# Moving two products of a later group of columns beside page building, with squares in PSUM, split exponentials and reordered pools

## The chip, the cores and the metric

The kernel runs on one core of one Trainium2 chip. A core has five engines with a queue of instructions each: TensorE (PE in the profile) multiplies matrices and transposes, VectorE (DVE), ScalarE (ACT) and GpSimd (POOL) work element by element, and SyncE (SP) issues most of the transfers. An engine works its queue in order: an instruction whose operand is not there yet holds up all that stand behind it. The metric is device microseconds (us) of one execution; lower is better. Before the change three runs gave 2585.85 to 2589.04 us, with a median of 2587.65 us.

## The reference

One layer of an encoder with 2048 tokens of 1024 features. In float32 throughout:

```python
h = rms_norm(x, norm_mix)
z = h @ w_in                       # 1024 x 4352: q_A k_A v_A q_B k_B v_B gate_A gate_B
y_a = windowed_gqa(q_a, k_a, v_a, sink)        # 8 heads, window |t-s| <= 128, ALiBi, a sink logit
y_b = neighborhood_attn(q_b, k_b, v_b, rpb)    # 8 heads on a 32 x 64 grid, 8 x 16 neighbours, bias
gates = sigmoid([g_a, g_b] + b_gate)
x = x + (gates[:, :1024] * (y_a @ w_proj_a) + gates[:, 1024:] * (y_b @ w_proj_b)) @ w_out
x = x + relu(rms_norm(x, norm_mlp) @ w_up) ** 2 @ w_down
out = rms_norm(x, norm_final)
```

## The kernel before

Tokens are worked in four blocks of 512. Every float32 operand of a product is split into a high and a low part (a cast on ACT writes the high part, a subtraction on DVE the low part, L309 and L310 in `split`), and a product is three passes on PE: high x high, high x low, low x high (`mm3s`, L313 to L315). So each operand that PE takes has one ACT cast and one DVE subtraction of its own ahead of it.

**The head, 0 to about 360 us.** The product `h @ w_in` of the first two blocks is done by a scheme with seven products in place of eight, numbered 1, 2, 5, 6, 7, 4, 3 in the order in which they are made (`ORDER`). The columns of `w_in` are taken in nine groups (`QUADS`, counted from 0; the code calls a group a quad): 0 is k_A and v_A, 1 is q_A, 2 is q_B, 3 is k_B, 4 is v_B, 5 to 8 are the gates. `in_quad` is a generator; each `next` makes one of the seven products of its group, into PSUM banks named x (products 1 and 2), z (5 and 3) and y (6, 7, 4). Product 1 is copied out as `c1` (tile zc, L514), and the result of product 2 is the first finished tile (q and k tiles are written as ze, L455 to L460).

The right-hand operands of the products are pages (tiles zh1 to zh7): pages 1 and 2 are the two halves of the first block's normalised, transposed tokens, page 3 belongs to the second block, and pages 5, 6, 7 and 4 are sums and differences of both. While the second block's pages are built (transposes on PE, L301; scaling on ACT, L534; four combining instructions on DVE, L537), only products 1 and 2 can run, since they need the first block alone. Before the change products 1 and 2 of groups 0, 1 and 2 run there; then come the products 5, 6, 7, 4 and 3 of groups 0 and 1, alternating; after that one group follows the other in a loop over q.

The weights come from DRAM: 1 MB halves (zraw, two tiles of four rotating buffers each) or, for group 2's first two products, 512 KB pieces loaded into buffers of the first block's token tiles (xin). `in_left` makes the sums and parts of the weights (zS, zwhl), ahead of the products that use them.

The norms: `rstd_shared` (blocks 0 and 1) sums the squares of half a row on ACT (L236) and of the other half on DVE (L238), with the squares themselves going to scratch tiles in SBUF; `rstd_of` (blocks 2 and 3, within groups 5 and 6) sums both halves on ACT with the squares going to the two PSUM banks of `tpool` (L250), adds them on DVE (L253) and takes the power on POOL (L255).

**Attention A, about 360 to 611 us.** Units of 128 queries of one key group; `turn` transposes a chunk of probabilities on PE, ACT casts it (tile ph, L874 or L879) and DVE makes the low part (L875 or L880); `product` multiplies it with v (tile av, L896). `score` of a unit three ahead multiplies q and k (L821), adds the bias and takes the maximum on DVE (L825), and after the fourth score ACT makes two small instructions and four exponentials of 288 columns (L829 to L832) in one row. DVE adds the sums and takes reciprocals (L833, L834), and POOL scales (L836). Between the chunks stand feature products of blocks 2 and 3 (mm, L203 to L205) as a filler, in steps of three matmuls, spread evenly by the constants `STEP` and `SCORE`.

**Attention B, from about 600 us.** The same pattern with units of 16 columns of the grid. Bias tiles biass0, biass1 and biasl are made on POOL from raw rows braw and the masks (L1033). Queries are loaded into qb0, qb1, qb2. The pools of B are laid on a stack of memory in the order of a list of names (L1007); a tile whose memory overlaps memory of A's tiles waits until these are done with. The scheduler keeps the order of the code within an engine except where `tc.issue_after` or priorities of the framework move an instruction behind another one.

## Time and profile before

| what | value |
|---|---|
| runs | 2585.85 to 2589.04 us, median 2587.65 us |
| the profiled execution | 2586.27 us, of which the span of the profile is 2584.4 us |
| PE busy | 2557.0 us, 99% of the span, 12200 instructions |
| DVE, ACT, POOL busy | 1610.0 us (62%), 1235.5 us (48%), 401.6 us (16%) |
| granted TensorE clock | 0.9 or more in all 40 slices of the page |
| DMA | 490.40 MB, mean 190 GB/s |

The page shows shares of the whole span. A view by windows gives the busy time of each engine in a stretch, a view of waits lists, for each engine, on which other engine's instruction its idle time ended, and the chain follows the work that ended last. Durations of matmuls in the views are longer than the distance from one start to the next, since matmuls are pipelined; where the prediction counts PE time it uses distances between starts.

### The profile page before, as it was taken

The page shows a single profiled execution, that of the slowest core. Times are in us where ns is not written, and L with a number is a line of the kernel's source. Part 1 is how long each engine was busy: PE and PEld are TensorE (multiplying, and loading weights), DVE is VectorE, ACT ScalarE, POOL GpSimd, SP SyncE. Part 2 cuts the span into 40 slices and gives each one's busy share as a digit, 9 for nine tenths or more (in the row PEclk, how much of TensorE's full clock was granted, in tenths as well). Part 3 has the DMA queues.
Part 4 walks back from the last instruction along what each step waited for, and adds up shares of the span by engine and source line. Part 5 has one row for each costly group of instructions (what it writes and reads, how often), then busy time and mean ns, then how long its engine had stood idle before and what let it go on. Part 6 is the DMA issues. An engine that isn't in the chain of part 4 may idle for free.

```text
span 2584.4 us, 34858 instructions
## 1 busy us (share of the span) xinstructions
PE 2557.0 (99%) x12200; PEld 2141.6 (83%) x12200; DVE 1610.0 (62%) x2625; ACT 1235.5 (48%) x2265; POOL 401.6 (16%) x613
## 2 busy tenths in 40 slices
PE   8999999999999999999999999999999999999999
PEld 6888888888888888888888888888888888888887
DVE  8776657765544445566578767866665535554766
ACT  5334347775555555443335554654454322323454
POOL 1000026665455541000000000100000000000010
PEclk9999999999999999999999999999999999999999
DMA  5657486467867647675457666844428835444555
GB/s 185 198 163 208 129 262 174 121 188 200 225 192 203 187 131 236 218 226 171 128 175 240 226 210 212 305 162 163 151 108 310 283 102 183 143 155 159 188 195 171
DMA packets 354127, 490.40 MB, mean 190 GB/s; under 512 B 28808, under 2 KB 188808, under 8 KB 351776
## 3 DMA queue, kind: packets, MB, share of 16 engines
q1 hardware_dynamic: 346896, 471.14, 58.4%
q10 hardware_dynamic: 7056, 17.04, 1.8%
q8 instruction: 96, 1.57, 0.3%
q14 instruction: 79, 0.65, 0.1%
HBM read 328.64 MB, written 159.45 MB: 189 GB/s over the span
## 4 chain that ended last, share of the span: by engine, by line
PE 87%; DMA 5%; DVE 4%; ACT 2%; issue 1%; SPq 1%; POOL 0%; ACTq 0%; POOLq 0%; DVEq 0%
PE b L313 16%; PE b L314 16%; PE b L315 16%; PE mm L203 5%; PE mm L205 5%; PE mm L204 5%; PE pt L203 2%; PE pt L204 2%; PE av L1128 2%; PE pt L205 2%; PE zb L315 2%; PE zb L313 2%; PE zb L314 2%; PE pt L1107 2%; PE s L1076 2%; PE av L896 1%
## 5 line engine op out<-in xcount | busy, mean ns | idle before, releaser
L314 PE MATMUL b<-dwh,dah 128*128 128x512 f32 x896 | 348.5, 389 | 0.0
L315 PE MATMUL b<-dwh,dah 128*128 128x512 f32 x896 | 347.6, 389 | 0.0
L313 PE MATMUL b<-dwh,dah 128*128 128x512 f32 x896 | 339.6, 389 | 0.0
L309 ACT CAST dah<-da 128x1024 fp32r<-128x1024 f32 (+1 forms) x128 | 120.9, 945 | 368.1 <-PE b L315 244.1
L310 DVE TENSOR_TENSOR dah<-da,dah 128x1024 fp32r<-128x1024 f32 (+1 forms) x128 | 139.5, 1090 | 223.4 <-ACT dah L309 223.3
L314 PE MATMUL b<-ubh,uwhlb 128*128 128x512 f32 x592 | 230.3, 389 | 0.0
L313 PE MATMUL b<-ubh,uwhlb 128*128 128x512 f32 x592 | 230.2, 389 | 0.0
L315 PE MATMUL b<-ubh,uwhlb 128*128 128x512 f32 x592 | 229.2, 389 | 0.0
L203 PE MATMUL mm<-hT,whl 128*128 128x512 f32 x544 | 218.5, 402 | 1.3 <-DVE zc L304 1.2
L205 PE MATMUL mm<-hT,whl 128*128 128x512 f32 x544 | 213.6, 393 | 0.0
L204 PE MATMUL mm<-hT,whl 128*128 128x512 f32 x544 | 213.1, 392 | 0.0
L313 PEld LDWEIGHTS b<-dwh,dah 128*128 128x128 f32 x896 | 168.2, 188 | 35.0
L314 PEld LDWEIGHTS b<-dwh,dah 128*128 128x128 f32 x896 | 168.2, 188 | 34.9
L315 PEld LDWEIGHTS b<-dwh,dah 128*128 128x128 f32 x896 | 168.2, 188 | 34.9
L313 PE MATMUL zb<-zh,zwhl 128*128 128x512 f32 x476 | 186.2, 393 | 5.2 <-DVE zh L537 1.6
L314 PE MATMUL zb<-zh,zwhl 128*128 128x512 f32 x476 | 185.8, 390 | 0.0
L315 PE MATMUL zb<-zh,zwhl 128*128 128x512 f32 x476 | 183.0, 390 | 1.7 <-DVE zwhl L310 1.7
L304 DVE TENSOR_TENSOR uc<-b,uc 128x512 f32<-128x512 f32 x160 | 109.1, 689 | 104.5 <-PE b L315 103.5
L1679 POOL TENSOR_TENSOR st<-st,power 128x1 f32<-128x1 f32 x16 | 13.4, 844 | 925.2 <-DVE st L1678 925.2
L313 PEld LDWEIGHTS b<-ubh,uwhlb 128*128 128x128 f32 x592 | 111.1, 188 | 23.5 <-issue 0.4
L314 PEld LDWEIGHTS b<-ubh,uwhlb 128*128 128x128 f32 x592 | 111.1, 188 | 23.1
L315 PEld LDWEIGHTS b<-ubh,uwhlb 128*128 128x128 f32 x592 | 111.1, 188 | 23.0
(269 smaller groups left out, 5883.1 us busy)
## 6 DMA issues: line engine op xcount, KB each, us to landing
at<-uc SPq DMA_DIRECT2D x224, 256.0 KB
da<-at SPq DMA_DIRECT2D x96, 512.0 KB
dw<-in_w_down_dram SPq DMA_DIRECT2D x160, 256.0 KB
uraw<-in_w_up_dram SPq DMA_DIRECT2D x32, 1024.0 KB
raw<-in_w_in_dram SPq DMA_DIRECT2D x34, 512.0 KB
zraw<-in_w_in_dram SPq DMA_DIRECT2D x16, 1024.0 KB
z<-zg SPq DMA_DIRECT2D x64, 256.0 KB
zg<-zc SPq DMA_DIRECT2D x32, 256.0 KB
```

What stands on the lines that cost most here:

```text
L203: PE.matmul(ps, lh, rh, start=first, stop=False)
L204: PE.matmul(ps, lh, rl, start=False, stop=False)
L205: return PE.matmul(ps, ll, rh, start=False, stop=last).ins
L304: return eng.tensor_tensor(out=out, in0=a, in1=b, op=op).ins
L309: casts.append(A.copy(hi, src).ins)
L310: return eng.tensor_tensor(out=lo, in0=src, in1=hi.bitcast(F32), op=ALU.subtract).ins
L313: PE.matmul(ps, lh, rh, start=first, stop=False, skip_group_check=True)
L314: PE.matmul(ps, lh, rl, start=False, stop=False, skip_group_check=True)
L315: PE.matmul(ps, ll, rh, start=False, stop=last, skip_group_check=True)
L1076: ins = PE.matmul(ps[:, :n], self.q[:, i, :], kv[:, z, B_R0[i] // 4 : (B_R0[i] + B_NR[i]) // 4, 4 * B_C0[j] : 4 * (B_C0[j] + w)], start=z ...
L1107: ins = PE.transpose(pt[:kp, at + (i - i0) * P : at + (i - i0 + 1) * P], self.s[i][:, rr : rr + kp], ident).ins
L1128: ins = PE.matmul(po[:, i0 * P : (i0 + ni) * P], self.v[:kp, c, :], src[:kp, o : o + ni * P], start=pair == x == z == 0, stop=(c == 7 and ...
```

## The change

Five edits.

1. In `rstd_shared` the squares go to the two PSUM banks of `tpool` in place of two SBUF scratch tiles, whose pools are dropped.
2. Products 1 and 2 of group 3 (the k_B columns) are made beside the second block's pages too: their two weight pieces are loaded early into xin buffers, product 1 after the pages' first half, product 2 after the second. Their `c1` tiles go to a ring zc3 of their own, which is kept until group 5.
3. In `rstd_of` the DVE addition of blocks 2 and 3 becomes two additions on POOL, with EPS held in a tile. In group 6 the squares of the last two token tiles are put behind the sixth weight cast, not the fifth.
4. In attention A the four exponentials of a unit are taken in two halves (`weigh`), each placed behind the cast and the low part of the chunk transposed next; the sums, reciprocals and scaling follow the second half.
5. In the list of B's pools qb1 and qb2 stand ahead of biass1.

```diff
     sink_t = cp.tile([P, AH], F32, name="sink_t")
-    power = cr.tile([P, 1], F32, name="power")
+    half = cr.tile([P, 2], F32, name="power")
+    power, eps = half[:, 0:1], half[:, 1:2]
     G.memset(power, -0.5)
+    G.memset(eps, EPS)
...
         st = T(pl, [P, 4], F32, "st", 4)
-        junk = T(pl, [P, 512], F32, "junk", 1)
+        junk = zbank(tpool, 2)
         A.activation(junk, t[:, 0:512], AF.Square, accum_out=st[:, 0:1])
-        other = T(pl, [P, 512], F32, "junkv", 1)
+        other = zbank(tpool, 2)
...
         r = st[:, 2 : 3]
-        V.scalar_tensor_tensor(out=r, in0=st[:, 0:1], scalar=EPS if mean else D * EPS, in1=st[:, 1:2],
-                               op0=ALU.add, op1=ALU.add)
+        if mean:
+            G.tensor_tensor(out=r, in0=st[:, 0:1], in1=st[:, 1:2], op=ALU.add)
+            G.tensor_tensor(out=r, in0=r, in1=eps, op=ALU.add)
+        else:
+            V.scalar_tensor_tensor(out=r, in0=st[:, 0:1], scalar=D * EPS, in1=st[:, 1:2], op0=ALU.add, op1=ALU.add)
...
     in_page[3] = ring(s_z, "zh3", PAGE, F32R, 2)
+    s_c = ExitStack()
+    in_c3 = ring(s_c, "zc3", [P, BT], F32, 2)
...
     kvw = ring(s_kv, "kvw", [P, 4, 256], F32, 2)
-    xp.update(pools(s_kv, "right", ("junk", "junkv", "st"), "x0"))
+    xp.update(pools(s_kv, "right", ("st",), "x0"))
...
-    def in_quad(c, w, lf, right, ybanks=ypool, zbanks=zpool):
+    def in_quad(c, w, lf, right, ybanks=ypool, zbanks=zpool, kept=None):
...
                 if n == 1:
-                    c1[a] = in_c()
+                    c1[a] = (kept or in_c)()
...
-    ops2 = []
-
-    def operands2():
+    ops = {2: [], 3: []}
+
+    def operands(q):
         while True:
-            yield ops2.pop(0)
-
-    quad2 = in_quad(*QUADS[2], operands2(), right)
-    for p in range(2):
-        t = T(xp, [P, D], F32, "xin", 8).rearrange("p (k c) -> p k c", k=4)
-        c = QUADS[2][0]
-        SY.dma_start(t, w_in[0][p * BT : (p + 1) * BT, c : c + 256].rearrange("(k p) f -> p k f", p=P))
-        ops2.append(left_parts(t, 256, V))
-        if p == 0:
-            with tc.issue_after(last_part[0]):
-                for o, h, l in zip(halves(t1), *map(halves, right[1])):
-                    add(V, o, h.bitcast(F32), l.bitcast(F32))
-        next(quad2)
+            yield ops[q].pop(0)
+
+    quads = {q: in_quad(*QUADS[q], operands(q), right, kept=in_c3 if q == 3 else None) for q in (2, 3)}
+    early = {}
+    for q in (2, 3):
+        c = QUADS[q][0]
+        for p in range(2):
+            t = T(xp, [P, D], F32, "xin", 8).rearrange("p (k c) -> p k c", k=4)
+            SY.dma_start(t, w_in[0][p * BT : (p + 1) * BT, c : c + 256].rearrange("(k p) f -> p k f", p=P))
+            early[q, p] = t
+
+    def first_two(q, p):
+        ops[q].append(left_parts(early[q, p], 256, V))
+        next(quads[q])
+
+    ops[2].append(left_parts(early[2, 0], 256, V))
+    with tc.issue_after(last_part[0]):
+        for o, h, l in zip(halves(t1), *map(halves, right[1])):
+            add(V, o, h.bitcast(F32), l.bitcast(F32))
+    next(quads[2])
+    first_two(2, 1)
...
                 page_parts(5, t1, V)
+                first_two(3, 0)
...
             scaled_less(l, ps, k, h.bitcast(F32))
+    first_two(3, 1)
...
             s_v.close()
+            s_c.close()
...
         del casts[:]
-        lf = list(in_left(ws, 256, (1, 2) if q == 2 else ()))
+        lf = list(in_left(ws, 256, (1, 2) if q in quads else ()))
...
                 normalised(xp, xt, Junk(), by_scalar=True)
-        ops2.extend(lf if q == 2 else ())
-        for n, _ in enumerate(quad2 if q == 2 else in_quad(*QUADS[q], iter(lf), right)):
+        if q in quads:
+            ops[q].extend(lf)
+        for n, _ in enumerate(quads[q] if q in quads else in_quad(*QUADS[q], iter(lf), right)):
             if q == 6 and n == 0:
-                for t, behind in zip(xt, 2 * [copied[0]] + 2 * [casts[4]]):
+                for t, behind in zip(xt, 2 * [copied[0]] + 2 * [casts[5]]):
...
+    cast, low = [None], [None]
+
+    def behind_parts():
+        both = ExitStack()
+        for ins in (cast[0], low[0]):
+            both.enter_context(tc.issue_after(ins))
+        return both
+
...
-        def score(self, u, forced=True):
+        def score(self, u, forced=True, later=False):
...
                                    scale=1.0, scalar=sink_g, op0=ALU.add, op1=ALU.max, accum_out=mx[:, u : u + 1])
-            if u < 3:
+            if u == 3 and not later:
+                self.weigh((0, 1))
+                self.weigh((2, 3))
+
+        def weigh(self, us):
+            s = self.s
+            mx, nm, sm, es, ri = (self.st[:, k, :] for k in range(5))
+            sink_g = sink_p[:, self.g : self.g + 1]
+            if us[0] == 0:
+                A.activation(nm, mx, AF.Copy, scale=-1.0)
+                A.activation(es, mx, AF.Exp, bias=sink_g, scale=-1.0)
+            for u in us:
+                lo, hi = self.span[u]
+                A.activation(s[:, u, lo:hi], s[:, u, lo:hi], AF.Exp, bias=nm[:, u : u + 1], accum_out=sm[:, u : u + 1])
+            if us[0] == 0:
                 return
-            A.activation(nm, mx, AF.Copy, scale=-1.0)
-            A.activation(es, mx, AF.Exp, bias=sink_g, scale=-1.0)
-            for u, (lo, hi) in enumerate(self.span):
-                A.activation(s[:, u, lo:hi], s[:, u, lo:hi], AF.Exp, bias=nm[:, u : u + 1], accum_out=sm[:, u : u + 1])
...
             if kind == "rest":
-                A.copy(ph[0:64, at], pt[0:64, at])
-                V.tensor_tensor(out=ph[64:P, at], in0=pt[0:64, at], in1=ph[0:64, at].bitcast(F32), op=ALU.subtract)
+                cast[0] = A.copy(ph[0:64, at], pt[0:64, at]).ins
+                low[0] = V.tensor_tensor(out=ph[64:P, at], in0=pt[0:64, at], in1=ph[0:64, at].bitcast(F32), op=ALU.subtract).ins
...
             pl = T(ap_, [P, 512], F32R, "pl", 2)
-            A.copy(ph[:, at], pt[:, at])
-            V.tensor_tensor(out=pl[:, at], in0=pt[:, at], in1=ph[:, at].bitcast(F32), op=ALU.subtract)
+            cast[0] = A.copy(ph[:, at], pt[:, at]).ins
+            low[0] = V.tensor_tensor(out=pl[:, at], in0=pt[:, at], in1=ph[:, at].bitcast(F32), op=ALU.subtract).ins
...
     chunks = [(n, c) for n, x in enumerate(units) for c in x.groups()]
-    behind, scored, begin = [], 0, given
+    behind, weighed, scored, begin = [], [], 0, given
...
         behind.append((x, c, x.turn(c)))
+        if weighed:
+            with behind_parts():
+                y, us = weighed.pop(0)
+                y.weigh(us)
...
             for u in {"middle": (0, 1), "outer": (2, 3), "rest": ()}[c]:
-                units[n + AHEAD].score(u)
+                units[n + AHEAD].score(u, later=True)
                 scored += 1
+                if u == 3:
+                    weighed = [(units[n + AHEAD], us) for us in ((0, 1), (2, 3))]
...
     s_b = ExitStack()
-    bp = pools(s_b, "right", ("masks", "kb0", "qb0", "braw0", "biass0", "stb", "biass1", "qb1", "qb2", "braw1", "biasl", "kb1"), "b")
+    bp = pools(s_b, "right", ("masks", "kb0", "qb0", "braw0", "biass0", "stb", "qb1", "qb2", "biass1", "braw1", "biasl", "kb1"), "b")
...
     last_exp, last_parts, n_raw, n_short = [None], [None], [0], [0]
```

The first place is the head, where DVE has finished the first half of the second block's pages. The names zh1, zh2 are pages of the first block, zh3, zh5, zh6, zh7 and zh4 those that need the second block; zwhl are parts of weights, xin here a weight piece of products 1 and 2, zb a PSUM bank. On PE before:

```order
L315 MATMUL zb_13_467<-zh2_27_245,zwhl_58_484 128x512
L313 MATMUL zb_24_642<-zh5_61_521,zwhl_74_626 128x512
L314 MATMUL zb_24_642<-zh5_62_522,zwhl_74_626 128x512
L313 MATMUL zb_23_629<-zh5_61_521,zwhl_74_626 128x512
L314 MATMUL zb_23_629<-zh5_62_522,zwhl_74_626 128x512
L315 MATMUL zb_23_629<-zh5_61_521,zwhl_74_626 128x512
```

And on PE now, behind the same last matmul of group 2's product 2:

```order
L320 MATMUL zb_29_471<-zh2_19_243,zwhl_44_486 128x512
L318 MATMUL zb_34_564<-zh1_17_241,zwhl_53_561 128x512
L319 MATMUL zb_34_564<-zh1_18_242,zwhl_53_561 128x512
...
L318 MATMUL zb_35_579<-zh1_17_241,zwhl_53_561 128x512
...
L318 MATMUL zb_34_564<-zh2_19_243,zwhl_56_630 128x512
...
L318 MATMUL zb_41_701<-zh5_47_523,zwhl_66_698 128x512
```

Where the products with page 5 followed at once, 48 matmuls of group 3 (with pages 1 and 2) now stand ahead of the first product with page 5. Its banks zb_34 and zb_35 are the x banks in which group 2's products lay, so that its first matmul takes the bank of zb_28 and its thirteenth that of zb_29. On DVE there, before:

```order
L537 SCALAR_TENSOR_TENSOR zh3_64_524<-zb_21_586,g_mix_68,zh3_63_523 128x512
L310 TENSOR_TENSOR zwhl_74_626<-zS_73_624,zwhl_74_626 128x1024
L304 TENSOR_TENSOR kvw_6_195<-kvw_6_195,zS_75_664 128x4x128
L310 TENSOR_TENSOR zh7_68_603<-zraw_30_304,zh7_67_602 128x1024
L456 TENSOR_TENSOR ze_59_499<-zb_12_452,ze_59_499 128x4x128
L304 TENSOR_TENSOR zraw_29_303<-zh2_27_245,zraw_29_303 128x1024
L456 TENSOR_TENSOR ze_60_516<-zb_13_467,ze_60_516 128x4x128
L310 TENSOR_TENSOR zwhl_76_666<-zS_75_664,zwhl_76_666 128x4x128
```

And now:

```order
L544 SCALAR_TENSOR_TENSOR zh3_50_526<-zb_39_621,g_mix_68,zh3_49_525 128x512
L463 TENSOR_TENSOR ze_45_501<-zb_28_456,ze_45_501 128x4x128
L315 TENSOR_TENSOR zh7_60_675<-zraw_22_302,zh7_59_674 128x1024
L309 TENSOR_TENSOR zraw_21_301<-zh2_19_243,zraw_21_301 128x1024
L463 TENSOR_TENSOR ze_46_518<-zb_29_471,ze_46_518 128x4x128
L315 TENSOR_TENSOR zwhl_64_680<-zS_63_678,zwhl_64_680 128x4x128
```

The first group's parts for page 5 (zwhl_66_698) have moved some ten rows back on DVE, and the reading of the x banks (ze_45, ze_46) two rows forward; that reading comes behind the four L544 instructions of the last two page tiles, as it did. Farther up, where before stood the low part of a page 5 weight (zwhl_608) and a sum (zS_75), DVE now makes the low parts of the two pieces, zwhl_53_561 and zwhl_56_630.

The second place is ACT in attention A, one unit's exponentials (sa is a unit's scores, sta its maxima and sums, ph the high part of a transposed chunk, ya an output). Before:

```order
L829 ACTIVATE sta_3553<-sta_3553 128x4
L830 ACTIVATE sta_3553<-sta_3553,byhead_2955 128x4
L874 CAST ph_3616<-pt_3615 64x512
L832 ACTIVATE sa_2974,sta_3553<-sa_2974,sta_3553 128x288 x4
L879 CAST ph_3643<-pt_3642 128x512
L904 COPY ya_3671<-av_136_3612 64x512
```

Now:

```order
L911 CAST ph_3613<-pt_3612 64x512
L863 ACTIVATE sta_3562<-sta_3562 128x4
L864 ACTIVATE sta_3562<-sta_3562,byhead_2964 128x4
L867 ACTIVATE sa_2983,sta_3562<-sa_2983,sta_3562 128x288 x2
L916 CAST ph_3644<-pt_3643 128x512
L867 ACTIVATE sa_2983,sta_3562<-sa_2983,sta_3562 128x288 x2
L941 COPY ya_3680<-av_152_3609 64x512
```

No cast of a chunk has more than two exponentials of a unit directly ahead of it now, and the rest chunk's cast stands ahead of the exponentials.

The third place is POOL at the passage from attention A to B (ve is the last copy of A, sb are B's probabilities being scaled, whl a weight part of the filler). Before:

```order
L852 COPY ve_6220<-va_294_2971 64x128 x2
L1033 TENSOR_TENSOR biass_787_7010<-braw_788_7011,masks_6374 128x288
L1033 TENSOR_TENSOR biass_787_7010<-braw_788_7011,masks_6374 128x384
L1096 TENSOR_SCALAR sb_706_6447<-sb_706_6447,stb_6443 128x288
L1096 TENSOR_SCALAR sb_707_6452<-sb_707_6452,stb_6443 128x384
L180 TENSOR_TENSOR whl_6486<-raw_6136,whl_6486 128x1024
L1033 TENSOR_TENSOR biasl_6433<-braw_702_6434,masks_6374 128x384
```

Now:

```order
L889 COPY ve_6229<-va_280_2980 64x128 x2
L1076 TENSOR_TENSOR biass_677_6397<-braw_678_6398,masks_6383 128x288
L1076 TENSOR_TENSOR biass_677_6397<-braw_678_6398,masks_6383 128x384
L182 TENSOR_TENSOR whl_6495<-raw_6145,whl_6495 128x1024
L1076 TENSOR_TENSOR biasl_6442<-braw_688_6443,masks_6383 128x384
L1076 TENSOR_TENSOR biass_715_6617<-braw_716_6618,masks_6383 128x288
L1139 TENSOR_SCALAR sb_692_6456<-sb_692_6456,stb_6452 128x288
```

Ahead of the second unit's scaling (sb_706 before, sb_692 now) POOL now has the second unit's own bias, a weight part, the third unit's wide bias and the next short bias, each of the biases three instructions.

## The prediction

> **What bounds the kernel now.** I read the page first, then the waits of PE, then windows of 20 us over the head, and last the chain and the rows of single engines at the places that the change touches. The page:

> ```profile
> PE 2557.0 (99%) x12200; PEld 2141.6 (83%) x12200; DVE 1610.0 (62%) x2625; ACT 1235.5 (48%) x2265; POOL 401.6 (16%) x613
> PEclk9999999999999999999999999999999999999999
> PE 87%; DMA 5%; DVE 4%; ACT 2%; issue 1%; SPq 1%; POOL 0%; ACTq 0%; POOLq 0%; DVEq 0%
> ```

> PE is busy for 99% of the span at a full clock, and it is 87% of the chain. The change removes no matmul, so all it can give is time in which PE stands. The waits of PE (engine and line, what it waited for, us in total, times, longest) say how much that is:

> ```profile
> PE zb L301 <- DVE xin L559: 7.9, 3, 7.2
> PE av L896 <- DVE ph L875: 2.8, 4, 2.0
> PE zb L315 <- DVE zwhl L310: 1.7, 2, 1.4
> PE zb L313 <- DVE zh L537: 1.6, 1, 1.6
> PE s L1076 <- DMA qb<-qs_b: 1.3, 1, 1.3
> PE zb L313 <- DVE ze L460: 1.3, 2, 0.9
> ...
> PE zb L313 <- ACT zc L514: 0.9, 1, 0.9
> ...
> PE zb L313 <- DVE st L253: 0.6, 1, 0.6
> ```

> The first row is the start of the kernel, before any token is normalised, and the change leaves it. The seven others are 10.2 us, 0.4% of the time; the change aims at each of them. A measurement of this kernel tells about 0.2% (5.2 us) from no change, so half of all that is to be had would be needed to be seen.

> Where PE stands in the head, the windows show why (PE, PEld, DVE, ACT, POOL busy us of 20):

> ```profile
> 20.00:40.00 20.00, 18.63 (x94) 15.13 (x95) 19.93 (x32) 13.37 (x25) 4.41 (x4) 1.00 0.45 123
> 40.00:60.00 20.00, 18.09 (x79) 14.33 (x78) 20.00 (x27) 9.06 (x12) 0.00 (x0) 1.00 0.33 88
> 60.00:80.00 20.00, 18.60 (x84) 15.09 (x84) 19.84 (x23) 6.82 (x8) 0.00 (x0) 1.00 0.54 175
> ```

> From 20 to 80 us DVE is never idle while PE has 1.4 to 1.9 us of gaps in each window. In this stretch DVE, not PE, sets the pace; work for PE alone does not help there unless its operands cost DVE nothing.

> **The change, part by part.**

> *Group 3's first two products beside the second block's pages.* They are 48 matmuls and take the place, on PE, of 48 matmuls with pages 5 and 6. Each piece needs one ACT cast and one DVE low part of 1024 columns. The rows of before around the two stalls:

> ```profile
> 50.30 0.39 PE L314 MATMUL zb<-zh,zwhl 128*128 128x512 f32 x1
> 52.26 0.47 PE L313 MATMUL zb<-zh,zwhl 128*128 128x512 f32 x1 [1.57 <-DVE zh L537]
> 53.30 0.50 PE L315 MATMUL zb<-zh,zwhl 128*128 128x512 f32 x1 [0.34 <-DVE zwhl L310]
> 65.92 0.50 PE L315 MATMUL zb<-zh,zwhl 128*128 128x512 f32 x1 [1.40 <-DVE zwhl L310]
> 52.03 1.22 DVE L310 TENSOR_TENSOR zwhl<-zS,zwhl 128x1024 fp32r<-128x1024 f32 x1
> 53.16 0.69 DVE L304 TENSOR_TENSOR kvw<-kvw,zS 128x512 f32<-128x512 f32 x1
> 53.76 1.22 DVE L310 TENSOR_TENSOR zh<-zraw,zh 128x1024 fp32r<-128x1024 f32 x1
> 54.90 0.69 DVE L456 TENSOR_TENSOR ze<-zb,ze 128x512 fp32r<-128x512 f32 x1
> 64.64 1.22 DVE L310 TENSOR_TENSOR zwhl<-zS,zwhl 128x1024 fp32r<-128x1024 f32 x1
> ```

> From start to start a DVE instruction of 1024 columns costs 1.14 us (52.03 to 53.16), one of 512 columns 0.60 us (53.16 to 53.76), and a matmul 0.228 us. On DVE the two low parts stand where two instructions of 512 columns stood, so the row after them, which began at 52.03, begins 2 x 0.54 us later, at 53.1. It is now the reading of the bank into which PE has to write group 3's product 1 (ze_45). That takes 0.7 us, so PE, which is through with group 2's product 2 at 50.08, goes on at about 53.85: a stand of 3.8 us where before there were 1.73 + 0.5 us (52.26 less 50.30 and one step of 0.23; and 53.30). The moved products do not fill this hole, because their bank is released by the same queue whose lateness makes the hole. After it 48 matmuls take 10.9 us, with 0.1 us for the second bank, which is read from 55.97 to 56.66, two instructions of 1024 columns later; PE then makes four matmuls and needs the low part of group 0's page-5 weights at 65.9. DVE gets there as follows: from 55.97 four instructions of 512 columns and six of 1024 make 9.2 us, so the low part runs from 65.2, and PE goes on at 66.4: 0.55 us, where before it was 1.56 us (65.92). Sum: 3.8 + 0.1 + 0.5 = 4.4 us against 3.8 us, so +0.6 us. The earlier stands of the head (the rows DVE ze and ACT zc of the waits) end on rows whose place on their queues has hardly changed, and I leave them.

> The lower end: DVE's rows keep their order but some could run without waiting for ACT; if the bank were free in time, the 3.8 us would go, which gives -3.2 us. The upper end lies in the next loads:

> ```profile
> 70.50 0.37 SPq L545 DMA_DIRECT2D zraw<-in_w_in_dram  x1
> 76.08 1.23 DVE L304 TENSOR_TENSOR zS<-zraw,zraw 128x1024 f32<-128x1024 f32 x1
> ```

> SP issues the second of group 2's halves at 70.50, and DVE's first sum of both begins at 76.08, so a load takes 5.6 us at the most. Now that sum stands ahead of a low part of group 1 on DVE (row zS_1005 ahead of zwhl_759), at about 71.5, while SP issues the second half only when DVE has finished page 4's second half, at about 68.3; with 5.6 us for a load it lands near 73.9, so DVE stands 2.4 us and zwhl_759 comes at 77.5, when PE needs it. I take 0; each us by which the load is later is 1 us of PE. Upper end +2.5.

> *Squares in PSUM.* Eight on ACT and eight on DVE, all ahead of the second block's pages.

> ```profile
> L236 ACT ACTIVATE junk<-xin 128x512 f32<-128x512 f32 x8 | 5.2, 646 | 4.7 <-DMA xin<-in_x_dram 4.7
> L250 ACT ACTIVATE zb<-xin 128x512 f32<-128x512 f32 x6 | 3.6, 592 | 3.9 <-DMA xin<-in_x_dram 3.9
> ```

> On ACT the same square into PSUM is 54 ns shorter, and ACT has room (13.37 of 20 us in the first window above). No row has a DVE square into PSUM; the nearest are 0.69 us for 512 columns read from PSUM (L456) and 0.69 us from SBUF (kvw, L304), so I take 0 for the term, with the 54 ns of ACT eight times, 0.4 us, to either side. [...]

> *The mean on POOL, the later squares.* The rows of group 6:

> ```profile
> 261.83 0.16 DVE L253 SCALAR_TENSOR_TENSOR st<-st 128x1 f32<-128x1 f32 x1 [1.17 <-ACT zb L250]
> 264.67 0.47 PE zb L313
> ```

> DVE stood 1.17 us for a square, ahead of a low part for which PE then waited (the 0.6 us row of the waits). With the addition off DVE, and the squares behind the next weight cast, that goes: -0.6. What it costs: two POOL additions in place of one DVE instruction, eight times.

> ```profile
> L242 POOL TENSOR_TENSOR st<-st,power x8: 550/931/1397, 5.7 to 26.7; 128x1 f32<-128x1 f32 x8
> L255 POOL TENSOR_TENSOR st<-st,power x24: 549/550/4806, 222.1 to 1373.5; 128x1 f32<-128x1 f32 x24
> ```

> One takes 0.55 us, and 0.93 to 1.4 beside a busy DVE, so a chain is 1.0 to 2.6 us longer. It ends in ACT's scaling of the tile, which the transposes to DRAM follow; PE does not read them in this stage. Cover is ACT's idle time; if an ACT cast behind such a scaling is late, 0.5 us. So -0.6 to +0.5.

> *Exponentials in halves.* The chain and rows of the longest stand in attention A:

> ```profile
> 571.15 1.13 ACT sa L832 x4
> 573.36 0.38 DVE L833 TENSOR_TENSOR sta<-sta 128x4 f32<-128x4 f32 x1 [2.07 <-ACT sa L832]
> 575.46 0.51 PE L896 MATMUL av<-ph,ve 128*128 128x256 f32 x2 [2.02 <-DVE ph L875]
> ```

> The rest chunk's cast (L874) stood behind four exponentials, and its low part (L875) behind a DVE sum (L833) that waited for the same four. Now the cast comes first, and the sum later. So the four stands of the waits row go: -2.8, at best -3.4 if the following gap steps go too. What is late next: a weight cast of 1.0 us on ACT, which can still stand ahead of a chunk's cast; with two exponentials (1.0 us) that makes 2 us, as before the exponentials alone did. A stand may thus come back at one or two of the four: upper end -1.0.

> *B's pools.* qb2 no longer lies where biass1 did, so its load starts in attention A, and the wait of 1.3 us goes. In exchange biass1 lies on memory of A, and is made only when A's last product is through.

> ```profile
> 604.62 3.06 POOL L1033 TENSOR_TENSOR biass<-braw,masks 128x288 f32<-128x288 f32 x3 [2.73 <-issue]
> 607.89 2.12 POOL L1096 TENSOR_SCALAR sb<-sb,stb 128x288 f32<-128x288 f32 x4 [0.21 <-DVE stb L1093]
> 612.86 2.40 POOL L180 TENSOR_TENSOR whl<-raw,whl 128x1024 fp32r<-128x1024 f32 x1 [2.85 <-ACT whl L179]
> 618.02 3.91 POOL L1033 TENSOR_TENSOR biasl<-braw,masks 128x384 f32<-128x384 f32 x3 [2.76 <-DMA braw<-tab]
> 611.56 0.34 PE pt L1107 x3
> 612.62 6.42 DMA qb<-qs_b
> ```

> A ends at 611.4. POOL then makes biass1 (3.06, to 614.5), the weight part (2.40, to 616.9), biasl (its raw rows landed at 618.0; 3.91, to 621.9), the next short bias (3.06, to 625.0) and the first scaling of the second unit (0.5, to 625.5). PE's transposes of that unit come after 30 feature matmuls at 0.23, 18 transposes at 0.11, 12 scores at 0.2 and 12 products at 0.12, 12.7 us, at 624.1. So PE stands 1.3 us: the gain is given back, and the term is 0, from -1.3 (raw rows earlier) to +2.

> **Sum** against the profiled execution of 2586.27 us, 1.4 us below the median: +0.6 + 0 - 0.6 - 2.8 + 0 = -2.8, so 2583.5 us, 0.16% below the median and within 0.2% of it.

> **The rivals.**
> *The head fills after all.* If the x banks are free in time, the 4.4 us of the hand sum go: 2586.3 - 3.8 - 0.6 - 2.8 = 2579, and with B's 1.3 us 2578. For it: the work is there. Against it: the bank is read on the busiest queue.
> *POOL's queue at the start of B* decides against the change. The work from A's end to the second unit's scaling is 12.9 us of POOL instructions; the profile has POOL's small instruction at 550 and at 931 to 1397 ns, 1.7 times and more, beside a busy DVE. At 1.7 times PE would stand 1.3 + 0.7 x 12.9 = 10.3 us: 2583.5 + 9 = 2592.5. It ends above before from 1.2 times on. Against it: L1033 in the rows above keeps to 3.06 us, and that was beside the DVE work of both attentions. [...]
> *Group 2's load holds DVE up*: landing 5 us after the hand sum, it costs 5 us: 2588.5.
> *The halves do not help*, since the weight cast takes their place: 2586.

> **How the numbers follow.** The forecast 0.42, the filled head 0.23, POOL's queue 0.12, the load 0.13, the halves 0.10. The forecast's own range is 2581 to 2587, by its larger ends taken singly. Faster by over 0.2% (below 2582.5) is most of the filled head, 0.21, and the lower end of the forecast, 0.07: 0.28. Slower by over 0.2% (above 2592.8) is most of POOL's queue, 0.08, and half of the late load where it meets the upper ends of the head and of B, 0.07, with 0.03 for the halves coming on top of either: 0.18. Within lies 0.54. The range of 2577.5 to 2591 leaves out the far end of the filled head and most of POOL's queue.

> **What would show it.** PE's matmul after the last of group 2's product 2 begins near 53.85 and its idle time ends on DVE's reading of a bank; a start at 51 would show the head filled. The row av <- ph gone from the waits shows the halves right. The wait for qb gone and one of about 1.3 us for POOL's sb in its place shows the start of B as summed. The prediction is wrong if DVE is idle between 68 and 76 us for more than 3 us, or if A has new waits.

## The result, and the profile after

The changed kernel is slower: a median of 2600.48 us (2599.09 to 2602.33) against 2586.75 us (2585.13 to 2589.04) for the kernel before, a ratio of 1.0049 with a 95% interval of 1.0036 to 1.0062. The prediction of 2583.5 us is missed by 17 us, and the time lies above the upper end of its range. The page of the changed kernel:

```profile
span 2600.5 us, 34864 instructions
PE 2563.5 (99%) x12200; PEld 2146.8 (83%) x12200; DVE 1606.6 (62%) x2617; ACT 1236.8 (48%) x2265; POOL 403.6 (16%) x630
```

PE still runs 12200 matmuls, but it is busy 6.5 us longer (2557.0 before) and stands some 9.6 us longer, which makes the 16.1 us by which the span grew from 2584.4 us. So two things have to be found: new stands, and matmuls that take longer. The waits of PE (engine and line, what it waited for, us in total, times, longest):

```profile
PE pt L1150 <- POOL sb L1139: 6.7, 2, 6.3
PE zb L320 <- DVE zwhl L315: 3.7, 2, 3.0
PE zb L318 <- DVE ze L463: 3.6, 1, 3.6
PE s L848 <- DVE sta L852: 1.9, 1, 1.9
```

The wait of the av matmuls for ph (2.8 us before) and the wait for qb (1.3 us) are gone. The rows in their place are larger: 6.7 us for POOL's sb at the start of attention B, 3.7 us for a weight part, 3.6 us for a bank, 1.9 us at the start of attention A.

To see what each place costs with the slower matmuls in it, I took for every matmul the distance from the start of the one before it, less the median of that distance for its shape, and added the excess up by stretches. The sum of these is PE's whole loss; its growth, 16.0 us, is that of the span.

| stretch of the changed kernel | loss before, us | loss after, us | difference |
|---|---|---|---|
| 0 to 40: start | 8.6 | 8.9 | +0.3 |
| 40 to 140: second block's pages and what follows | 5.0 | 10.0 | +5.0 |
| 220 to 360: groups 5 to 8 | 2.9 | 2.6 | -0.3 |
| 360 to 400: start of attention A | 0.9 | 5.0 | +4.1 |
| 400 to 600: rest of attention A | 5.7 | 2.8 | -2.9 |
| 600 to 680: start of attention B | 2.2 | 11.0 | +8.8 |
| after 1000 | 1.6 | 2.6 | +1.0 |

The stretches that the table leaves out lost the same before and after. Below, "stand" means such an excess at one matmul.

**The head.** PE around the first stand, start and duration in us:

```profile
50.20 0.39 PE L320 MATMUL zb<-zh,zwhl 128*128 128x512 f32 x1
54.14 0.80 PE L318 MATMUL zb<-zh,zwhl 128*128 128x512 f32 x1 [3.55 <-DVE ze L463]
54.74 0.63 PE L319 MATMUL zb<-zh,zwhl 128*128 128x512 f32 x1
55.16 0.63 PE L320 MATMUL zb<-zh,zwhl 128*128 128x512 f32 x1
```

The stand for the bank is there, 3.71 us where 3.8 were summed. What was not summed stands right behind it: six matmuls come 0.43 us apart, where 0.23 us is usual. The windows give the granted clock (the column PEclk, the third from the end) over these matmuls and over those that follow:

```profile
54.00:57.30 3.30, 3.16 (x8) 2.48 (x9) 3.30 (x5) 0.20 (x1) 0.00 (x0) 0.50 0.58 137
58.00:62.00 4.00, 4.00 (x19) 3.33 (x18) 4.00 (x5) 1.54 (x2) 0.00 (x0) 1.00 0.75 154
```

The half clock over these 3.3 us cost 1.2 us. On the page the slices are 65 us long, and every digit of PEclk is a 9. The stand of 1.56 us at 65.9 is gone, and a second one has come at 81.56, of 3.16 + 0.37 us with 1.16 us of slower matmuls. DVE ahead of it:

```profile
77.88 1.23 DVE L309 TENSOR_TENSOR zS<-zraw,zraw 128x1024 f32<-128x1024 f32 x1 [5.20 <-issue]
...
80.29 1.22 DVE L315 TENSOR_TENSOR zwhl<-zS,zwhl 128x1024 fp32r<-128x1024 f32 x1
```

DVE is idle for 5.20 us ahead of the sum of group 2's two weight halves, and the low part that PE waits for stands two instructions behind that sum. SP issued the second half at 69.06:

```profile
69.06 0.63 SPq L552 DMA_DIRECT2D zraw<-in_w_in_dram  x1
```

So 8.8 us passed from the issue to the start of the sum, where the prediction had 5.6 us for the load.

**The start of attention B.** POOL's rows for three of the short biases (a time in brackets is idle time ahead of the row), then SP's issues of the raw rows that they are made from:

```profile
617.47 3.05 POOL L1076 TENSOR_TENSOR biass<-braw,masks 128x288 f32<-128x288 f32 x3 [11.10 <-PE av L933]
...
643.36 3.04 POOL L1076 TENSOR_TENSOR biass<-braw,masks 128x288 f32<-128x288 f32 x3 [6.85 <-DMA braw<-tab]
...
669.50 2.96 POOL L1076 TENSOR_TENSOR biass<-braw,masks 128x288 f32<-128x288 f32 x3 [14.40 <-DMA braw<-tab]
```

```profile
636.49 0.62 SPq L1070 DMA_DIRECT2D braw<-tab  x1
...
646.42 0.60 SPq L1070 DMA_DIRECT2D braw<-tab  x1
...
659.18 4.10 SPq L1070 DMA_DIRECT2D braw<-tab  x1
```

Up to about 633 us POOL goes by the prediction's own chain: biass1 only after A's last product, a weight part, biasl, the next short bias, the second unit's scaling (sb, at 630.33). PE's stand for that scaling is 0.84 us at 630.9 (1.3 us were summed); 0.48 us at 624.9, for a bank that DVE reads, come beside it. Then it goes on. POOL is idle from 636.5 on, until the raw rows that SP issues at 636.49 have landed; SP's next raw load may go only when POOL has read its buffer, at 646.4, and all transfers after it in SP's order (keys, queries, weights, values) wait with it; the raw load behind these goes out at 659.18, and POOL stands 14.4 us for it. The end of the chain:

```profile
659.18 10.19 DMA braw<-tab
...
673.00 1.01 PE pt L1150 x3
```

PE stands 6.5 us here, 0.5 us follow at the next two steps, and 2.2 us go to a clock of a half that lasts until 678.5. Before, the raw load at that place went out at 645.47, 13.7 us earlier, while A's end had been only 6.1 us earlier (611.4 against 617.5); the bias was made just in time, with a stand of 0.3 us.

**The start of attention A.** At 381.02 a stand of 2.03 us with 1.85 us of slower matmuls, which the prediction did not have at all. The chain goes through a transfer:

```profile
372.68 6.42 DMA zg<-zc
```

And the rows of ACT and PE behind it:

```profile
379.21 0.60 ACT L466 ACTIVATE z<-mm 128x512 fp32r<-128x512 f32 x1 [7.50 <-DMA zg<-zc]
...
381.02 1.20 PE L848 MATMUL s<-ka,qa 128*128 128x288 f32 x4 [1.86 <-DVE sta L852]
```

ACT had to wait 7.5 us for a gate tile (zc) to be written to DRAM before it could write a z tile into that memory. That write, issued at 372.68, took 6.42 us. DVE's read of the z product and then the maxima of a unit's scores stood behind it, and with them the score bank that PE needs.

### The profile page after: what moved, and what is told of

The parts are those of the page before. It is cut to its first block, busy times and chain, and to the rows that moved or that the text cites. A ratio compares the mean times of both kernels' runs of the same rounds, so it can differ in the third digit from the quotient of the medians.

```text
span 2600.5 us, 34864 instructions
## 1 busy us (share of the span) xinstructions
PE 2563.5 (99%) x12200; PEld 2146.8 (83%) x12200; DVE 1606.6 (62%) x2617; ACT 1236.8 (48%) x2265; POOL 403.6 (16%) x630
## 3 DMA queue, kind: packets, MB, share of 16 engines
q8 instruction: 96, 1.57, 0.3%
## 4 chain that ended last, share of the span: by engine, by line
PE 81%; DMA 4%; DVE 2%; ACT 1%; issue 1%; POOL 0%; SPq 0%; POOLq 0%; ACTq 0%; DVEq 0%
PE b L318 15%; PE b L320 15%; PE b L319 15%; PE mm L207 5%; PE mm L205 5%; PE mm L206 5%; PE pt L205 2%; PE pt L206 2%; PE pt L207 2%; PE av L1171 2%; PE pt L1150 2%; PE s L1119 2%; PE av L933 1%; PE s L848 1%; PE pt L908 1%; PE zb L318 1%
## 5 line engine op out<-in xcount | busy, mean ns | idle before, releaser
L314 ACT CAST dah<-da 128x1024 fp32r<-128x1024 f32 (+1 forms) x128 | 120.9, 945 | 367.3 <-PE b L320 247.5
L315 DVE TENSOR_TENSOR dah<-da,dah 128x1024 fp32r<-128x1024 f32 (+1 forms) x128 | 139.5, 1090 | 222.6 <-ACT dah L314 222.4
```

Source lines behind the costliest of these rows:

```text
L314: casts.append(A.copy(hi, src).ins)
L315: return eng.tensor_tensor(out=lo, in0=src, in1=hi.bitcast(F32), op=ALU.subtract).ins
```

## The experiments

Each result is the ratio to the kernel before, run on the same chip beside it. Three kernels (the turned ring and the two with stands made on purpose) have one time only, and are read by their traces.

### The old list of pools

```diff
-    bp = pools(s_b, "right", ("masks", "kb0", "qb0", "braw0", "biass0", "stb", "qb1", "qb2", "biass1", "braw1", "biasl", "kb1"), "b")
+    bp = pools(s_b, "right", ("masks", "kb0", "qb0", "braw0", "biass0", "stb", "biass1", "qb1", "qb2", "braw1", "biasl", "kb1"), "b")
```

> The changed kernel with B's list of pools as it was before (biass1 ahead of qb1 and qb2). Theory: the pools' order alone makes the stands of PE at the start of B (0.48 and 0.84 us near 625 and 631, 6.5 us at 673 with 2.2 us of slower matmuls behind it). They go, the wait of 1.3 us for qb comes back: 2600.5 - 9.9 + 1.4, about 2592 us. Rival: the exponentials in halves, which put POOL's scaling later, make them; then the stand of 6 us stays and the time is 2600 to 2602.

Measured: 2592.06 us, a ratio of 1.0022 (1.0013 to 1.0031). The stand at 673 is gone, and the wait for qb is back:

```profile
PE s L1119 <- DMA qb<-qs_b: 2.7, 1, 2.7
```

with 0.6 us after it and 2.65 us of slower matmuls. The stands at the start of A are 0.59 us and less here. So the 6.5 us at 673 hang on the reordered list. The head's two stands are as in the changed kernel (3.74 and 2.89 us).

### The head as before

```diff
-    quads = {q: in_quad(*QUADS[q], operands(q), right, kept=in_c3 if q == 3 else None) for q in (2, 3)}
+    quads = {q: in_quad(*QUADS[q], operands(q), right, kept=None) for q in (2,)}
...
-                first_two(3, 0)
...
-    first_two(3, 1)
```

> The changed kernel without group 3's early products (no early loads, no ring zc3; squares in PSUM stay). Theory: the stands at 54 us (3.7 + 0.4) and 81.6 us (3.2 + 0.4), with 2.4 us of slower matmuls behind them, give way to those of before (1.7 + 0.5 + 1.6): -6.2. The stand of 2.0 us at 381, with 1.9 us behind it, waits for a write out of a zc buffer, and the zc ring turns by two places less where c1 lies in zc3; so it goes as well: -3.9, in sum about 2590.5 us. Rival: the stand at 381 is the halves' work; it stays, about 2594.5. Rival: the squares in PSUM slow the head; then PE's stands up to 70 us stay over 5 us.

Measured: 2591.22 us, 1.0017 (1.0008 to 1.0025). The first two stands in the head are those of before (1.72 and 0.50 us at 52 to 53; here with 1.55 us of slower matmuls); the third one, of 1.56 us at 65.9, is gone, with PE coming to that place later by about as much. The one at 81 is gone, and so is the one at the start of A. The one in B stays (6.16 us, with 2.2 us of slower matmuls). Against the changed kernel this is -9.3 us, and the rows of the table for the head and for the start of A have 9.1 us between them.

### Both undone

```diff
...
-                first_two(3, 0)
...
-    first_two(3, 1)
...
-    bp = pools(s_b, "right", ("masks", "kb0", "qb0", "braw0", "biass0", "stb", "qb1", "qb2", "biass1", "braw1", "biasl", "kb1"), "b")
+    bp = pools(s_b, "right", ("masks", "kb0", "qb0", "braw0", "biass0", "stb", "biass1", "qb1", "qb2", "braw1", "biasl", "kb1"), "b")
```

> The changed kernel with the head of e2 (no early products of group 3) and B's old list of pools: squares in PSUM, the mean on POOL, the later squares and the halves stay. Theory: the costs of the two undone parts add up, 2591.2 of e2 less the 9.9 us at the start of B, plus about 1.5 to 2.5 for the wait for qb that e1 and e4 have: about 2583.5 us, with no stand over 2.5 us behind the first 20 us. Rival: the parts are not independent and a stand comes back elsewhere: 2587 or more.

Measured: 2583.92 us, 0.9989 (0.9980 to 0.9997). What is left of the change, the halves, the mean on POOL, the later squares and the squares in PSUM, is slightly faster than the kernel before. The two parts undone one at a time gave -8.4 and -9.3 us, both together -16.6 us: they add up to within 1.1 us, and are the whole slowdown.

### The sum of group 2's halves later

```diff
-        lf = list(in_left(ws, 256, (1, 2) if q in quads else ()))
+        lf = list(in_left(ws, 256, (1, 2) if q in quads else (), [last_part[0]] if q == 2 else None))
```

The sum that waits for the load is put behind group 1's low part on DVE.

> The changed kernel with the sums of group 2's weights put behind the last low part of groups 0 and 1 on DVE. Theory: the stand at 81.6 us is DVE's queue held by a sum whose load lands at 77.8 (5.2 us idle), ahead of the low part that PE needs. It goes, with its slower matmuls: -4.7, about 2596 us; the stand at 54 us stays at 3.7. Rival: DVE has too much work there in any order, by the two low parts and two results moved ahead (3.6 us); then a stand of 2 us or more is left between 70 and 90 us.

Measured: 2593.85 us, 1.0025 (1.0014 to 1.0035). DVE now:

```profile
76.34 1.23 DVE L315 TENSOR_TENSOR zwhl<-zS,zwhl 128x1024 fp32r<-128x1024 f32 x1 [4.55 <-ACT zwhl L314]
```

The low part comes at 76.34 in place of 80.29, and from 60 to 140 us PE loses nothing. So the second stand of the head came from the load ahead of that low part, as shown by taking it away. The first stand is unchanged (3.74 us, this time with 2.53 us of slower matmuls), and so is the one in B (6.84 us). The stand at the start of A went too, though nothing was changed there; ACT's wait of 7.5 us is replaced by one for PE itself:

```profile
373.14 0.60 ACT L466 ACTIVATE z<-mm 128x512 fp32r<-128x512 f32 x1 [4.79 <-PE mm L207]
```

### The raw rows loaded by another queue

```diff
-            SY.dma_start(raw, src)
+            (SY if n_raw[0] < 3 else G).dma_start(raw, src)
```

The new list of pools stays; from the third on, POOL itself issues the loads of raw rows, so that SP's other transfers do not stand behind a wait for POOL.

> The changed kernel with the loads of the bias' raw rows (all but the first two) issued by POOL, which reads them, and not by SP. Theory: the stand of 6.5 us at 673 comes from a ring of waits: SP stands for POOL (buffer braw free), POOL for the load, and the loads behind it on SP stand too. With POOL issuing, SP is free, the raw rows come sooner, and the stands from 620 to 680 us fall from 10.5 us with the slower matmuls to under 4: 2594 to 2596 us. Rival: the bias tile on A's memory starts the lateness and keeps it, whoever issues: the stand of 6 us stays, about 2600.

Measured: 2592.44 us, 1.0020 (1.0010 to 1.0029). The short bias that POOL made at 669.50 in the changed kernel, and the scaling behind which PE stood:

```profile
647.81 3.06 POOL L1076 TENSOR_TENSOR biass<-braw,masks 128x288 f32<-128x288 f32 x3 [3.06 <-DMA braw<-tab]
...
658.44 2.12 POOL L1139 TENSOR_SCALAR sb<-sb,stb 128x288 f32<-128x288 f32 x4
```

The stand of 6.5 us is gone. What is left from 620 to 680 us are four steps of 0.4 to 0.9 us, 2.3 us in all, without slower matmuls. With the order of the pools unchanged, and the same biases to be made after A's end, taking the raw loads out of SP's queue takes 8 us away: the ring of SP and POOL, and not POOL's work, made the loss. (The move also placed two of the short biases one scaling later or earlier in POOL's queue; the loads' place is not all that differs.)

### The old head with the raw rows on the other queue

```diff
...
-                first_two(3, 0)
...
-    first_two(3, 1)
...
-            SY.dma_start(raw, src)
+            (SY if n_raw[0] < 3 else G).dma_start(raw, src)
```

> The head of e2 (no early products of group 3), the changed list of B's pools (qb1 and qb2 ahead), the raw rows issued by POOL as in e9, and the squares, the mean and the halves as changed. Theory: e8 has 4.4 us of stands at the start of B (the wait for qb and slower matmuls), e9 has 3.0; the rest is that of e8: about 2582.5 us, and the wait for qb gone. Rival: e8's and e9's B cost the same in time, 2584; or the lateness of the first bias shows more when PE comes earlier: 2586.

Measured: 2583.48 us (2581.81 to 2585.59), 0.9986 (0.9977 to 0.9995). This is the change without its first part and with the ring broken. The first row of B among its waits of PE:

```profile
PE s L1114 <- DVE stb L1121: 1.2, 2, 0.9
```

No row for qb or sb stands ahead of it in that list. It and the kernel with both parts undone are the fastest of this study, 0.14% and 0.11% below the kernel before. Their intervals overlap, so even with the ring broken the new list of pools is not shown to be worth more than the old one.

### The halves alone

The diff is the part of the change from `cast, low` to `weighed`, on the kernel before.

```diff
...
+    cast, low = [None], [None]
...
+        if weighed:
+            with behind_parts():
+                y, us = weighed.pop(0)
+                y.weigh(us)
```

> The kernel before with the exponentials in halves alone. Theory: the four stands of attention A that ended on the low part of the rest chunk (3.4 us) go and nothing new comes: 2586.3 - 3.3, about 2583 us, and no stand near 381. Rival: the halves bring the stand at 381 us and its slower matmuls (3.9): about 2587. Rival: the halves bring the POOL stand of B: over 2590.

Measured: 2586.2 us, 0.9997 (0.9988 to 1.0006). ACT around the place where the longest stand was:

```profile
569.13 0.57 ACT L892 CAST ph<-pt 64x512 fp32r<-64x512 f32 x1
...
570.93 0.57 ACT L897 CAST ph<-pt 128x512 fp32r<-128x512 f32 x1
```

The rest chunk's cast comes ahead of all exponentials, the next chunk's after two, 1.80 us later. Of the four stands in A (0.39, 0.37, 0.48 and 2.18 us) one of 0.35 us is left: -3.1 us. But the wait for qb at the start of B grew:

```profile
PE s L1100 <- DMA qb<-qs_b: 2.2, 1, 2.2
```

From 1.3 to 2.2 us, since A ends earlier and the load of qb does not; and the stand for POOL's sb that was of 0.30 us at 660.68 is now of 0.80 us, at 657.82. So the span fell by 2.0 us (2582.4 against 2584.4), and the median by 0.7 us, which the interval does not tell from nothing.

### The mean on POOL and the later squares alone

```diff
+        if mean:
+            G.tensor_tensor(out=r, in0=st[:, 0:1], in1=st[:, 1:2], op=ALU.add)
+            G.tensor_tensor(out=r, in0=r, in1=eps, op=ALU.add)
...
-                for t, behind in zip(xt, 2 * [copied[0]] + 2 * [casts[4]]):
+                for t, behind in zip(xt, 2 * [copied[0]] + 2 * [casts[5]]):
```

> The kernel before with the mean of blocks 2 and 3 on POOL and the later squares alone. Theory: the stand of 0.8 us near 265 is not removed but changes its cause: DVE no longer waits for a square, but its transposes wait for the longer chain on POOL (three instructions of 0.55 us for one of 0.16 and one of 0.55) and ACT's scaling behind it, ahead of the sum that PE waits for: within 0.5 us of before. Rival, the prediction's term: -0.6 us and no stand over 0.3 us between 255 and 275.

Measured: 2586.16 us, 0.9996 (0.9987 to 1.0005). DVE no longer waits for a square there, but

```profile
265.53 0.77 DVE L279 STREAM_TRANSPOSE ze<-xin 128x256 f32<-128x256 f32 x2 [2.37 <-ACT xin L267]
266.23 0.65 DVE L309 TENSOR_TENSOR zc<-zb,zc 128x512 f32<-128x512 f32 x1
```

it waits 2.37 us for the scaling of the tile, which comes later with the squares; behind its two transposes stands the copy that frees a bank, and PE stands 0.80 us, where it was 0.77 us.

### The squares in PSUM alone

```diff
-        junk = T(pl, [P, 512], F32, "junk", 1)
+        junk = zbank(tpool, 2)
...
-        other = T(pl, [P, 512], F32, "junkv", 1)
+        other = zbank(tpool, 2)
...
```

> The kernel before with the squares of the first two blocks in PSUM alone. Theory: nothing (0 +- 0.4 us): the DVE squares take 0.69 us in PSUM as in SBUF, PE's first 40 us keep their stands. [...]

Measured: 2587.61 us, 1.0000 (0.9991 to 1.0009). PE loses 8.4 us in the first 40 us, where it was 8.6 us. The part is worth nothing that the runs show, either way.

### The ring of gate tiles turned by two

```diff
+        if q == 3:
+            for _ in range(2):
+                G.memset(in_c()[:, 0:1], 0.0)
```

Two tiles of the zc ring are written in one column and not used, so that from group 4 on each gate tile lies in another buffer: what the part zc3 had moved is moved back.

> The changed kernel with the zc ring turned on by two places ahead of group 3 (POOL writes one column of two tiles that nobody reads), as it was when c1 of group 3 lay in it. Theory: the first z tiles of the next stage take the memory of zc tiles; the stand of 2.0 us at 381 with 1.9 us behind it waits for a write out of a zc tile that the turned ring leaves to an earlier place; it goes: about 2596.5 us. Rival: that wait is a matter of when the write was issued and of the load on the DMA engines; e3, with the same ring as the changed kernel, has no such stand, and here it may stay or go.

Measured: 2601.2 us. The stand at the start of A stays, with 2.19 us:

```profile
PE s L851 <- DVE sta L855: 2.0, 1, 2.0
```

So it is not the place in the ring that makes it. The kernels with a stand of 2 us there (the changed one, this one, and the one with raw rows on POOL) have a write of gates that takes 6.35 us or more; in those without it, that write had landed in time. What makes the write long was not found. From 372.7 to 379.1 us the DMA engines are full in the changed kernel:

```profile
372.70:379.10 6.40, 6.35 (x31) 4.97 (x29) 2.10 (x9) 0.00 (x0) 1.12 (x2) 1.00 1.02 276
```

a share of 1.02 (the last column but one); but in the kernel with the sum later, in which the stand is gone, the share is 0.91 at that place. That a full queue is the cause is thus only argued.

### Stands made on purpose

```diff
...
+    def stand(count, rt, ps):
+        d = sd()
+        V.tensor_scalar(d[:, 0:1], ps[:, 0:1], 0.0, 0.0, ALU.mult, ALU.mult)
+        for _ in range(count):
+            G.tensor_tensor(out=d[:, 0:1], in0=d[:, 0:1], in1=d[:, 0:1], op=ALU.add)
+        lo = rt[:, 1, 0:1]
+        V.scalar_tensor_tensor(out=lo, in0=lo.bitcast(F32), scalar=d[:, 0:1], in1=lo.bitcast(F32), op0=ALU.mult, op1=ALU.add)
...
+                if (n, k) in stands:
+                    stand(stands[n, k], rt, banks[group[-1]])
```

On the kernel before, at 20 places of the last product, a chain of 2 to 7 small POOL additions of zeros is put ahead of a low part that PE needs; the result stays the same. A second kernel has 6 to 11 additions.

> The kernel before with 20 stands put into the last product stage (1560 us on), in five of its seven products at four places each: the low part of a right-hand operand waits for a chain of 2 to 7 POOL instructions of 0.55 us that starts at the partial sum of the step before (nothing of the result changes). Theory: the length of a stand alone makes the matmuls behind it run at 0.43 instead of 0.23 us: never below 1.5 us, always over 3.5 us, and in between by chance of its place; each such stand costs 1.2 to 2.5 us more. Rival: the slower matmuls belong to the places in the head and in the attentions (transfers, DVE's load); then none of the 20 has them. Sum of the stands about 20 x 3 us: 2645 to 2660 us, 2670 to 2690 with the slower matmuls.

Measured: 2617.92 us. An addition took 0.37 us and not the 0.55 us of the expectation, so the stands came out shorter. Stands of 0.4 to 2.3 us came, none of which was followed by slower matmuls, and two of 5.6 us, one right behind the other (5.65 and 5.63), with matmuls 0.43 us apart after the second, which cost 1.36 us.

The unchanged part of this kernel tells as much. The stand of 2.18 us at the end of attention A is the same in both traces, in the kernel before at 575.46 and here at 575.02. First the window of the kernel before, then that of this one:

```profile
575.00:579.00 4.00, 3.54 (x23) 3.12 (x23) 3.25 (x8) 1.97 (x6) 2.56 (x7) 1.00 0.10 19
```

```profile
575.00:579.00 4.00, 3.98 (x15) 3.60 (x16) 2.97 (x7) 2.14 (x7) 2.10 (x6) 0.57 0.17 34
```

The same stand at the same place is followed by a full clock in one execution and by 0.57 of it in another, where it costs some 1.5 us more.

> As the run with 20 stands, with 6 to 11 POOL instructions in a stand (0.37 us each there), so stands of about 2.5 to 4.6 us. Theory: with a length alone deciding by where it falls in some fixed period, nearly all stands over 3.5 us are followed by matmuls at 0.43 us, for 1.2 to 2.5 us of loss, and part of those of 2 to 3.5 us. Rival: only stands at places with many transfers or transposes have it: none of the 20.

Measured: 2669.4 us. With 6 to 11 additions there are 20 stands in one kernel, each of 1.67 to 6.71 us, and one more of 5.65 us. Slower matmuls, worth 1.1 to 2.4 us each time, followed on 15 of the 20. They followed on none of the three stands of 1.67 to 1.70 us, and on some of those between 1.97 and 2.5 us (on 1.97 and 1.98 at 2234.7 and 2377.2, but not on 1.98 at 2092.3; on 2.51 and 2.52, but not on 2.48 at 2277.0). Those from 2.7 us up were all followed by them, the one of 5.65 us by the next stand first. So a stand of 2 us or more can cost 1.1 to 2.4 us on top of its length.

What decides between two stands of about the same length is where they fall. In each trace the stretches at half clock begin on one grid of 3.41 us and last one step of it, or a whole number of steps: here they begin at 2112.36, 2132.84 and 2173.80, for example, 6 and 12 steps apart. Windows laid on the grid, first around the stand of 2.25 us that ends at 2111.00, then around the longer one of 2.48 us that ends at 2276.99:

```profile
2108.95:2112.36 3.41, 1.36 (x6) 1.14 (x7) 1.37 (x3) 0.00 (x0) 1.51 (x4) 1.00 0.43 153
2112.36:2115.77 3.41, 3.41 (x10) 2.63 (x9) 0.00 (x0) 0.00 (x0) 0.00 (x0) 0.50 0.00 1
2115.77:2119.19 3.42, 3.42 (x17) 2.79 (x16) 1.48 (x2) 1.57 (x2) 0.00 (x0) 1.00 0.00 0
...
2272.79:2276.20 3.41, 1.88 (x9) 1.23 (x7) 2.00 (x3) 1.57 (x2) 2.54 (x7) 1.00 0.71 257
2276.20:2279.61 3.41, 2.62 (x11) 2.17 (x12) 0.82 (x2) 0.00 (x0) 0.39 (x2) 1.00 0.66 216
```

The shorter stand lies almost whole in one step, in which PE is idle for 2.05 us (3.41 less 1.36), and the step behind it is at half clock. The longer one is cut by a border of the grid into 1.53 us and 0.79 us of idle time, and the clock stays full. The stand at the end of attention A shows the same, in the kernel before and in the one with 2 to 7 additions:

```profile
571.46:574.87 3.41, 1.98 (x14) 1.50 (x12) 1.48 (x7) 2.82 (x10) 2.69 (x2) 1.00 0.65 162
```

```profile
572.00:575.42 3.42, 1.40 (x9) 0.93 (x8) 2.44 (x8) 1.84 (x6) 2.70 (x4) 1.00 0.62 153
575.42:578.83 3.41, 3.41 (x13) 3.03 (x12) 2.55 (x7) 1.97 (x6) 1.68 (x6) 0.50 0.19 37
```

In the kernel before, PE is idle for 1.43 us of this step (3.41 less 1.98), and the clock stays full; in the other it is idle for 2.02 us, and the next step is at half clock. Over all 14 traces of this study, from 30 us after the start to 8 us before the end, a half clock came behind every step at full clock in which PE was idle for 1.86 us or more (35 of 35), behind 3 of 5 with 1.70 to 1.81 us, and behind none with less. The ends of matmuls are modelled in a profile, so the limit is not known to better than that. The grid did not lie at one place relative to the kernel's start (a step begins at 571.46 in the one trace and at 572.00 in the other), so that the same stand fell into it differently and cost more in one of the two.

## Why the prediction was wrong

**B's pools: summed as 0, from -1.3 to +2; it was +8.8 in the trace.** This is the step that failed most. Its beginning was right: POOL's queue was followed from A's end to the second unit's scaling, and of the 1.3 us of stand that it gave 0.84 us are there, in place of the wait for qb. The step that failed is where the following ended. The prediction took the raw rows as landing at times read from the trace before. But raw rows go through two buffers that POOL must have read before SP may load them again, and SP's other loads stand behind each such load in its queue. So POOL's lateness becomes SP's (which issues nothing from 639.8 to 646.4 us), SP's becomes that of keys, queries and values, and then again POOL's: PE's large stand is at 673, 42 us behind the one to which the prediction had followed the queue. The kernel with the loads on POOL's own queue shows it: the 6.5 us of stand gone, with the list of pools as it was and only the raw loads and what the framework moved with them changed. The rival "POOL's queue at the start of B" had the right engine and, at 10.3 us, about the right price, by a wrong mechanism: no instruction of POOL took longer (biass 3.05, biasl 3.92 us, as before); it waited.

**The head: summed as +0.6; it was +5.0.** The bank's stand was right within 0.1 us (3.71 against 3.8), and the low part of the page-5 weights ran at 65.48, where 65.2 was summed. That PE did not wait for it (0 against 0.55 us) is luck: PE came to it 1.6 us later than summed, by the slower matmuls (1.20 us) and 0.37 us at the second of them. The term "I take 0" for group 2's load failed: the 5.6 us taken for a load as "at the most" was the time of another load, at another moment, and this one took up to 8.8 us. The prediction's own signs named it (DVE idle for more than 3 us between 68 and 76: it was idle for 5.20 us, up to 77.9), and its upper end of +2.5 was too low by 1 us. That DVE set the pace there was right: 48 matmuls moved onto PE's idle time gained nothing, since their operands and their banks went through the same queue. In the kernel with the sum later, where the load's stand is gone, the head is still 1.6 us behind that of before (6.6 against 5.0 us): its 2.53 us of slower matmuls are more than that.

**What was no term of the sum: the clock after a stand.** Four stands of the changed kernel (54, 82, 381 and 673 us) are followed by matmuls at half the clock, which cost 1.20, 1.16, 1.85 and 2.16 us, 6.4 us of the 16. The page's digits, all 9, hide it. The prediction counted a stand as its own length; these four, of 2.03 to 6.5 us, cost 1.16 to 2.16 us more.

**What was no term either: the start of A.** 2.03 us, and 1.85 us with the clock. The change moves times by some us ahead of this place, and a write of gates then lands late (6.42 us after its issue at 372.68). It comes and goes with edits far away, why that write is long stays open, and the place was not in the working at all. It falls under the sign "new waits in A".

**The halves: -2.8 summed, -3.1 measured in A.** Right in mechanism and size; the fear of a weight cast in their place did not come true. But the sum took them as time gained at the end, and alone they gave the span 2.0 us, since the wait for qb grew by 0.9 us and a stand for POOL's sb by 0.5 us: what is gained ahead of a load's fixed moment is in part given back there.

**The mean and the later squares: -0.6 summed, 0 measured.** The additions cost less than taken (0.19 us each, 0.27 us from start to start in the chain, not 0.55). The part that failed is "PE does not read them in this stage": PE does not, but DVE's transposes of the scaled tile stand ahead of a bank's copy in DVE's queue.

**The squares: 0 summed, 0 measured.** On ACT 602 ns against 632 ns (medians of eight), a gain of 30 ns each where the prediction read 54; DVE's own rows are in the last section.

Against this, the gains were as small as the prediction had them: with the two failed parts undone, the kernel came to 2583.92 us, 0.11% under the kernel before.

## What to carry to other kernels

When a moved buffer makes one instruction late, follow the lateness through every ring that the instruction closes (the load that waits for its buffer, and all that stands behind that load in its queue) until some slack takes it up, and not only to the first engine that waits. Price a stand of PE of about 2 us or more at more than its length (here 1.1 to 2.4 us more, when most of it fell into one step of the clock's grid), and look at the granted clock in windows of a few us, since a page's slices hide it. A load's time in another place of the trace was no upper bound for it here (at most 5.6 us in one place, up to 8.8 us in the other): an instruction that waits for a load should not stand in an engine's queue ahead of what the bounding engine needs next.

## What the runs showed of the hardware that was not expected

*A square into PSUM is hardly dearer in itself on DVE, but reading its sum is.* The square and the reading of the accumulator, eight of each, first before (SBUF), then after (PSUM); min/median/max in ns:

```profile
L238 DVE CUSTOM_DVE_ANT_0 junkv<-xin x8: 681/687/693, 4.5 to 24.3; 128x512 f32<-128x512 f32 x8
L238 DVE DVE_READ_ACCUMULATOR2_ANT st<- x8: 81/84/86, 5.1 to 24.9; 128x1 f32 x8
```

```profile
L240 DVE CUSTOM_DVE_ANT_0 zb<-xin x8: 692/694/701, 4.5 to 24.6; 128x512 f32<-128x512 f32 x8
L240 DVE DVE_READ_ACCUMULATOR2_ANT st<- x8: 140/142/143, 5.2 to 25.2; 128x1 f32 x8
```

7 ns for the square and 58 ns for the reading behind it, 0.5 us for all eight; no time of a kernel shows it.

*The issue of a transfer itself can take long.* SP's issue of raw rows took 0.62 us at 636.49 and 4.10 us at 659.18, with keys, queries and values just issued ahead of it and the DMA engines at a share of 1.14 from 659.0 to 663.4. It comes on top of the 13.7 us by which that issue began late, and no engine's wait names it.
